# Softmax reciprocals on GpSimd as a power of minus one, and the two halves of the attention values added in place

## The chip, the cores and the metric

The kernel runs on one core of a Trainium2 chip. The metric is the device time of one execution in microseconds (us). TensorE is called PE, VectorE DVE, ScalarE ACT, GpSimd POOL, and SyncE, which issues the DMAs here, SP.

## The reference

One encoder layer on 1024 tokens with 1024 features, in float32: a conditioned RMSNorm, an input projection, two kinds of attention side by side (8 heads of latent attention, where a query sees all keys up to its own chunk of 64, and 8 heads of chunk attention, where it sees 9 chunks and a bias by relative position), an output projection, and a gated feed-forward part with a causal convolution. What the change touches is the softmax and what follows it, in both kinds of attention:

```python
    s = jnp.where(mask[None, None], s, NEG_INF)
    p = jax.nn.softmax(s, axis=-1).astype(v.dtype)
    return jnp.einsum('bqhk,bkhd->bqhd', p, v)
```

## The kernel before, in words

The work has four stages: the norm and the first projections (up to about 105 us of the span), attention with the other projections as filler (to about 670 us), the output projection (to about 745 us), and the feed-forward part. Every float32 matrix product is made of three products of high and low parts; the high part is a rounded copy made by ACT (L75), and the low part, the remainder, is made by POOL or DVE (L82).

Attention runs over 128 tiles. A tile is 128 queries of one head against all their keys (128 to 1024 of them); four tiles of a head form a unit. The 64 tiles of chunk attention come first (names with c: Pc, ric, hlc, PTc, pvc), then the 64 of latent attention (names with m). The method `scores` (L633) makes one tile:

- PE makes the scores in PSUM (L655), DVE their row minimum (L670 or L674; the sign is turned), and ACT the exponentials P with the row sum rsum beside them (L681).
- DVE makes ri, the reciprocal of rsum (L683), and scales it by 2^15 (L684).
- POOL makes the high half of the scaled probabilities in 16 bits, hl (L71, called at L702), and DVE the low half (L705). Rows of over 512 keys in latent attention are done in two pieces.
- SP issues a DMA that transposes hl into PT (L710).

Three tiles later the method `values` (L714) multiplies PT with the values in PE (L721). High and low parts of the values stand side by side, so the product pv has them on two halves of its 128 rows. After a unit's fourth tile ACT copies one half, scaled, from PSUM into the scratch tile sb (L728), DVE scales the other and adds sb to it into dst (L729), and SP stores dst (L730). Tiles sb and dst have one buffer each, rsum and ri four.

The filler is a list of generators that the loop over tiles (L822) runs between `scores` and `values`, by estimated costs: the other projections (L386, L395, L472), the two groups of latent up-projections (f_up, L517, with norms whose roots POOL makes as a power of -0.5: L115 and L116), and the output projection's half for chunk attention (f_oca, L595, whose weights and inputs are the tiles wo and cl). The program order so written is a proposal only: a list scheduler places the instructions of each engine and of SP's queue by data dependences, buffers and priorities, with modelled times (L1146). The scores have a higher priority (OFF_S) than the steps from the reciprocal on (OFF_P, L682) and the values (OFF_V). Within an engine the resulting order is fixed: an instruction that waits holds up all behind it.

## Time and profile before

| what | value |
|---|---|
| time, median of 3 runs | 1456.5 us (1454.95 to 1457.18) |
| the profiled execution | 1456.23 us, its span 1454.4 us |
| granted PE clock, mean | 0.936 |
| L683, L684 on DVE | 128 instructions each, medians 0.14 to 0.16 us |
| L71 on POOL | 160 instructions, 111.0 us |
| L728 on ACT, L729 on DVE | 32 each, medians 0.684 and 0.750 us |

All times in the views are counted from the span's start. A row of a group gives the source line, engine, operation, tiles written and read, shapes, the count, busy time and mean, then the engine's idle time before them and who ended it. A row of a source line gives shortest, median and longest duration in ns and the first and last start. A row of a wait gives who waited for whom, the us in total, the number of times and the longest. A row of the timeline gives start, length, engine, line, operation, and in brackets the idle time before it. A row of windows gives a stretch, its length and the busy time of each engine with the number of instructions, or of the instructions of one line alone.

### The profile page before, as it was taken

Reading aid. Unit: us, or ns where it says so; the run is one execution under the profiler, and the core shown is the slowest. Engines: PE = TensorE matmul, PEld = TensorE weight load, DVE = VectorE, ACT = ScalarE, POOL = GpSimd, SP = SyncE. Lnnn points to the kernel's source line nnn. Section 1 sums busy time; section 2 is a strip of 40 time slices with the busy share of each in tenths; the row PEclk is TensorE's granted clock in tenths of the full one; section 3 lists DMA queues with packets and bytes.
Section 4 is the critical chain, followed back from the end, with each engine's and each line's share of the span. In section 5 each row is a group of like instructions: output and inputs, shape, how many; then the busy total and the mean of one; then the engine's idle time right before and its main releaser. Section 6 shows DMA issues by size and latency. Waiting matters only on the chain.

```text
span 1454.4 us, 20116 instructions
## 1 busy us (share of the span) xinstructions
PE 1270.4 (87%) x6836; PEld 1054.4 (72%) x6836; DVE 1029.9 (71%) x1838; ACT 606.5 (42%) x1182; POOL 770.3 (53%) x717
## 2 busy tenths in 40 slices
PE   3859988998877789886668999999999998999997
PEld 2749877887765568675546877888888887887885
DVE  6964776576688988782577778778777776566653
ACT  4544344334455555452374343443444433322331
POOL 5363544265545764333735655556655555665662
PEclk9979997999887799997878999999999999999999
DMA  7423547555522588778712322322222234447442
GB/s 283 135 70 77 130 107 144 133 119 118 114 59 55 107 162 171 149 145 261 243 41 87 116 88 101 107 82 87 88 87 87 96 130 152 152 142 241 146 145 101
DMA packets 214627, 183.85 MB, mean 126 GB/s; under 512 B 148214, under 2 KB 179066, under 8 KB 213500
## 3 DMA queue, kind: packets, MB, share of 16 engines
q1 hardware_dynamic: 214524, 182.56, 45.3%
q8 instruction: 54, 0.88, 0.3%
q14 instruction: 49, 0.40, 0.1%
HBM read 119.07 MB, written 28.84 MB: 102 GB/s over the span
## 4 chain that ended last, share of the span: by engine, by line
PE 23%; POOL 9%; DVE 8%; issue 8%; DMA 7%; ACT 1%; SPq 1%; DVEq 0%; POOLq 0%; ACTq 0%
PE p L929 5%; PE p L931 5%; PE p L930 5%; POOL wds L82 5%; DMA wu<-w_up 2%; PE dnp L1072 2%; PE dnp L1074 2%; PE dnp L1073 2%; DVE u L1007 1%; DMA wd<-w_down 1%; DVE ws L1020 1%; DVE u L1006 1%; POOL wf L82 1%; POOL we L82 1%; POOL wd L82 1%
## 5 line engine op out<-in xcount | busy, mean ns | idle before, releaser
L82 POOL TENSOR_TENSOR wds<-wd,wds 128x512 fp32r<-128x512 f32 x88 | 152.4, 1753 | 102.7 <-ACT wds L75 102.7
L82 POOL TENSOR_TENSOR wc<-ws,wc 128x512 fp32r<-128x512 f32 x22 | 65.2, 2962 | 136.7 <-ACT wc L75 136.7
L1062 DVE TENSOR_TENSOR wd<-wd,gmbc 128x1024 f32<-128x1024 f32 x44 | 68.5, 1556 | 84.1 <-DMA wd<-w_down 84.0
L1074 PE MATMUL dnp<-wds,g 128*128 128x512 f32 x308 | 119.3, 393 | 4.6 <-DVE g L82 4.6
L1072 PE MATMUL dnp<-wds,g 128*128 128x512 f32 x308 | 120.0, 392 | 1.8 <-DVE xo L1080 1.7
L75 ACT ACTIVATE wds<-wd 128x512 fp32r<-128x512 f32 x88 | 54.8, 624 | 159.1 <-PE dnp L1074 152.3
L1073 PE MATMUL dnp<-wds,g 128*128 128x512 f32 x308 | 120.1, 391 | 0.0
L71 POOL TENSOR_SCALAR hlm<-Pm,rim 128x512 f16<-128x512 f32 (+3 forms) x96 | 64.8, 685 | 78.9 <-DVE rim L684 39.7
L71 POOL TENSOR_SCALAR hlc<-Pc,ric 128x640 f16<-128x640 f32 (+2 forms) x64 | 46.2, 724 | 80.6 <-DVE ric L684 39.5
L1020 DVE TENSOR_TENSOR ws<-wu,wu 128x512 f32<-128x512 f32 x22 | 30.5, 1387 | 75.0 <-DMA wu<-w_up 75.0
L681 ACT ACTIVATE Pc<-sc,mc 128x640 f32<-128x640 f32 (+2 forms) x64 | 42.2, 660 | 91.0 <-DVE mc L670 64.1
L655 PE MATMUL sm<-mk,mq 96*128 96x512 f32 (+3 forms) x288 | 71.2, 377 | 10.2 <-ACT Pm L681 6.7
L1006 DVE SCALAR_TENSOR_TENSOR u<-c,pk,u 128x1023 f32<-128x1023 f32 x44 | 77.4, 1766 | 1.8 <-ACT u L1005 1.8
L1041 ACT ACTIVATE u<-u 128x1024 f32<-128x1024 f32 x22 | 23.4, 1063 | 132.1 <-DVE u L1007 132.1
L655 PE MATMUL sc<-k,q 64*128 64x512 f32 (+3 forms) x288 | 68.7, 365 | 10.7 <-ACT Pc L681 6.8
L82 DVE TENSOR_TENSOR g<-gr,g 128x512 fp32r<-128x512 f32 x44 | 69.8, 1588 | 11.2 <-ACT g L75 11.2
L430 DVE SCALAR_TENSOR_TENSOR aacc<-aw,cs,aacc 128x256 f32<-128x256 f32 x84 | 44.1, 525 | 47.3 <-DMA aw<-w_ada 47.0
L1005 ACT ACTIVATE u<-c,pk 128x1024 f32<-128x1024 f32 x44 | 52.3, 1236 | 56.1 <-DVE c L1037 56.1
L705 DVE SCALAR_TENSOR_TENSOR hlm<-Pm,rim,hlm 128x512 f16<-128x512 f32 (+3 forms) x96 | 68.5, 727 | 6.1 <-POOL hlm L71 5.9
L721 PE MATMUL pvm<-PTm,vt 128*128 128x128 f16 x576 | 47.2, 232 | 28.6 <-DMA PTm<-hlm 24.5
L1074 PEld LDWEIGHTS dnp<-wds,g 128*128 128x128 f32 x308 | 58.2, 189 | 18.0 <-DVE g L82 5.9
L1072 PEld LDWEIGHTS dnp<-wds,g 128*128 128x128 f32 x308 | 58.1, 189 | 15.1 <-DVE xo L1080 2.6
(366 smaller groups left out, 4281.1 us busy)
## 6 DMA issues: line engine op xcount, KB each, us to landing
wu<-w_up SPq DMA_DIRECT2D x44, 512.0 KB, 4.5
wd<-w_down SPq DMA_DIRECT2D x44, 512.0 KB, 5.1
aw<-w_ada SPq DMA_DIRECT2D x96, 128.0 KB, 2.4
g_d<-u SPq DMA_DIRECT2D x22, 512.0 KB, 2.6
gr<-g_d SPq DMA_DIRECT2D x44, 256.0 KB, 3.6
x<-x SPq DMA_DIRECT2D x16, 512.0 KB, 6.6
adaw<-w_ada_a SPq DMA_DIRECT2D x8, 1024.0 KB, 5.2
wq_r<-w_qk SPq DMA_DIRECT2D x32, 128.0 KB, 2.8
```

The lines of the kernel that those rows point to most:

```text
L71: pool.tensor_scalar(o, i, s, 1.0, op0=MUL, op1=MUL)
L82: (pool if eng == "p" else dve).tensor_tensor(o, i, f32(hi), op=SUB)
L655: last = pe.matmul(s[:, c:c + w], qpg[rs_, a, q], kpgs[kh][rs_, b, ko:ko + w], start=(a == 0 and b == 0), stop=(a == 1))
L705: dve.scalar_tensor_tensor(hl[:, w:2 * w], pp, ri[:], hl[:, :w], op0=MUL, op1=SUB)
L929: pe.matmul(pt, sh, pg[:, 0], start=(k == 0), stop=False)
L930: pe.matmul(pt, sh, pg[:, 1], start=False, stop=False)
L931: pe.matmul(pt, sl, pg[:, 0], start=False, stop=(k == 3))
L1006: dve.scalar_tensor_tensor(u[:, 1:], c[:, :S - 1], pk[:, cv + 1:cv + 2], u[:, 1:], op0=MUL, op1=ADD)
L1062: dve.tensor_tensor(raw[:], raw[:], gmbc[:], op=MUL)
L1072: pe.matmul(pts[t][n], sh, w[n][:, 0], start=(j == 0), stop=False)
L1073: pe.matmul(pts[t][n], sh, w[n][:, 1], start=False, stop=False)
L1074: pe.matmul(pts[t][n], sl, w[n][:, 0], start=False, stop=(j == NF - 1))
```

## The change

The reciprocal is no longer made by DVE. POOL scales the row sum by 2^-15 and raises it to the power of -1, with a tile of -1 made once at the start. And ACT writes its half of the values straight into dst, to which DVE then adds the other half in place; the tile sb is gone. The scheduler places all instructions of the attention part anew; the numbers of lines shift by two from L102 on, and by one after the place where sb stood.

```diff
+    minus1 = cst.tile([P, 1], F32, name="minus1")
+    pool.memset(minus1[:], -1.0)
...
             with tc.high_priority(offset=OFF_P):
-                dve.reciprocal(ri[:], rsum[:, 0:1])
-                dve.tensor_scalar(ri[:], ri[:], PSCALE, None, op0=MUL)
+                pool.tensor_scalar(ri[:], rsum[:], 1.0 / PSCALE, 1.0, op0=MUL, op1=MUL)
+                pool.tensor_tensor(ri[:], ri[:], minus1[:], op=ALU.pow)
...
-                    sb = at.tile([P, 512], F32, name=f"sb{u.nm}_{u.g}", tag="sb", bufs=1)
                     dst = at.tile([P, 512], F32, name=f"o{u.nm}_{u.g}", tag="o", bufs=1)
                     r0, r1 = (slice(64, 128), slice(0, 64)) if u.odd else (slice(0, 64), slice(64, 128))
                     inv = vscale[u.vs][1]
-                    act.activation(sb[r0], u.pv[r1], AF.Copy, scale=inv[r1])
-                    dve.scalar_tensor_tensor(dst[r0], u.pv[r0], inv[r0], sb[r0], op0=MUL, op1=ADD)
+                    act.activation(dst[r0], u.pv[r1], AF.Copy, scale=inv[r1])
+                    dve.scalar_tensor_tensor(dst[r0], u.pv[r0], inv[r0], dst[r0], op0=MUL, op1=ADD)
                     sp.dma_start(u.dst_d[r0, u.g * 512:(u.g + 1) * 512], dst[r0])
```

## The prediction

> **What bounds the kernel now.** The page first: it says which engines are full on average.

> ```profile
> PE 1270.4 (87%) x6836; PEld 1054.4 (72%) x6836; DVE 1029.9 (71%) x1838; ACT 606.5 (42%) x1182; POOL 770.3 (53%) x717
> ```

> TensorE carries the kernel, but the diff touches only the attention part, and an average over the span says little of it. So I read busy time by stage next. The columns after the stretch and its length are PE, PEld, DVE, ACT and POOL, then granted clock, DMA share and GB/s.

> ```profile
> 105.00:405.00 300.00, 276.32 (x1965) 242.95 (x1964) 195.08 (x576) 124.88 (x335) 145.87 (x219) 0.93 0.54 117
> 405.00:435.00 30.00, 22.28 (x105) 16.95 (x104) 25.83 (x88) 15.94 (x40) 11.84 (x12) 0.83 0.25 56
> 435.00:520.00 85.00, 61.90 (x360) 49.49 (x361) 78.09 (x236) 47.36 (x111) 57.84 (x57) 0.82 0.43 93
> 520.00:670.00 150.00, 121.97 (x895) 100.59 (x892) 112.70 (x276) 70.04 (x148) 61.96 (x83) 0.93 0.80 160
> ```

> There are three stages. From 105 to 405 us (chunk attention with its projections) PE is busy 276.3 of 300 us: it bounds. From 435 to 520 us (latent attention together with its up-projections) DVE is busy 78.1 of 85 us, 92%, and PE only 61.9: DVE bounds, with POOL third at 57.8. From 520 to 670 us PE leads with 122.0 of 150 and nothing is full. The view of waits says how the reciprocal stands in this:

> ```profile
> POOL hlm L71 <- DVE rim L684: 39.7, 21, 4.8
> POOL hlc L71 <- DVE ric L684: 39.5, 18, 7.1
> ...
> PE pvm L721 <- DMA PTm<-hlm: 24.5, 19, 3.7
> ```

> POOL stands 79.2 us in all before its scaling of the probabilities (L71), until DVE has made the scalar ri; PE stands 24.5 us for the transposed probabilities that come of it. A tile in the timeline shows why:

> ```profile
> 493.65 1.01 ACT L681 ACTIVATE Pm<-sm,mm 128x896 f32<-128x896 f32 x1
> 493.75 0.15 DVE L683 RECIPROCAL rim<-rsm 128x1 f32<-128x1 f32 x1
> ...
> 498.81 0.14 DVE L684 TENSOR_SCALAR rim<-rim 128x1 f32<-128x1 f32 x1
> 498.88 0.27 DVE L467 TENSOR_TENSOR uqr<-qn,tabq 128x128 f32<-128x128 f32 x1
> 499.05 1.32 POOL L71 TENSOR_SCALAR hlm<-Pm,rim 128x512 f16<-128x512 f32 x2 [1.28 <-DVE rim L684]
> ```

> In DVE's order, 5 us of other work stand between one reciprocal and the next scaling. The same rows give the true price of such an instruction on DVE: L684 is recorded with 0.14 us, but the next instruction starts 0.07 us after it. Taking one away frees 0.07 us, not 0.15.

> **The change part by part.** The rows of the reciprocal in the three stages give the numbers of tiles:

> ```profile
> 105.00:405.00 300.00, 10.06 (x64) 0.93 0.54 117
> ...
> 435.00:520.00 85.00, 2.98 (x20) 0.82 0.43 93
> 520.00:670.00 150.00, 6.67 (x44) 0.93 0.80 160
> ```

> *Removed from DVE:* L683 and L684, 128 times each: 256 x 0.07 = 18 us of issue, of which 20 x 0.14 = 2.8 us in the stage that DVE bounds. The hop DVE to POOL goes too.

> *Added to POOL:* 128 times a scaling and a power, both 128x1. Before has no power of -1, but a power of -0.5 by the same instruction, and small scalings of the same kind:

> ```profile
> L115 POOL TENSOR_SCALAR ss<-ss x24: 191/198/1183, 79.8 to 741.4; 128x8 f32<-128x8 f32 x16, 128x1 f32<-128x1 f32 x8
> L116 POOL TENSOR_TENSOR rx<-ssx,nhalf x8: 549/551/566, 6.3 to 18.3; 128x1 f32<-128x1 f32 x8
> ...
> L344 POOL TENSOR_TENSOR vsm<-vsm,nhalf x2: 720/956/1191, 403.0 to 445.5; 128x1 f32<-128x1 f32 x2
> ...
> 435.00:520.00 85.00, 7.86 (x10) 0.82 0.43 93
> ```

> The low end is 0.19 + 0.55 = 0.74 us a tile. The last row is L115 (a scaling of 128x8) in the stage that matters: 7.86 / 10 = 0.79 us, four times its lowest. The power of 128x1 took 0.72 us at 445.5 and 1.19 us at 403.0. So the high end is 0.79 + 1.19 = 1.98 us, and I take the nearest rows by place, 0.79 + 0.72 = 1.51 us a tile from 435 to 520. The timeline shows POOL's instructions one after another with no overlap, so the price counts in full. The wait for the exponential's sum moves to POOL with it: behind it in POOL's order now stand the weights' remainders (L82), for which PE waits, and the up-projections' norms (L115, L116), for which DVE's L574 waits.

> [...]

> *Chunk attention, 64 tiles.* POOL would go from 145.9 to 145.9 + 64 x 1.51 = 242.5 of 300 us at most: still below PE's 276.3, and 39.5 us of POOL's waiting for ric go away. Value 0; bounds -3 (some of PE's 23.7 us of idle) to +4.

> *435 to 520 us, 20 tiles.* POOL gets 57.84 + 20 x 1.51 = 88.0 us of work in a stage that lasts 85: it takes DVE's place as the bound. If it idles as little as DVE does now (85 - 78.1 = 6.9 us), the stage lasts 94.9, or 9.9 us more. Some POOL work there can slide behind 520 us, where POOL has 88 us of room:

> ```profile
> L82 POOL TENSOR_TENSOR wo<-wor,wo 128x512 fp32r<-128x512 f32 x6 | 9.3, 1550 | 1.5 <-ACT wo L75 1.5
> ...
> L82 POOL TENSOR_TENSOR cl<-cl,ch 128x512 fp32r<-128x512 f32 x1 | 1.3, 1277 | 0.1
> ```

> If all 10.6 us slide, the stage ends 0.7 us early; if none, 9.9 late. The changed program's order on POOL keeps these between the tiles much as before, so I take the middle: +5. With the low price POOL has 72.6 us, DVE stays the bound and its 2.8 us come off: -3. With the high price POOL has 97.4 and the stage gains 19.

> *520 to 670 us, 44 tiles.*

> ```profile
> POOL hlm L71 <- DVE rim L684: 36.1, 19, 4.8
> ...
> PE pvm L721 <- DMA PTm<-hlm: 14.6, 11, 3.1
> ```

> POOL waited 19 times, 1.9 us each, for rim. At 0.79 to 1.51 us for the pair, a tile that waited gains 0.4 to 1.1 us (7.6 to 21 us in all) and the other 25 lose 0.8 to 1.5 us (20 to 38 us); POOL has 88 us free, so neither is the length of the stage. What counts is PE's 14.6 us of waiting for PTm. Value 0, bounds -6 (less than half of that goes) to +4.

> *The order.* The scheduler places things anew, in the attention part alone; from the feed-forward part on, the order is the same. One move stands out at the end: the loads of the first w_up page (SP, L938) and the two POOL remainders of it (wa, wb) go ahead of the last four tiles' scalars, and the first output-weight page (wo), which stood among those tiles, goes behind them.

> ```profile
> 652.56 2.37 POOL L71 TENSOR_SCALAR hlm<-Pm,rim 128x512 f16<-128x512 f32 x3 [2.36 <-DMA wor<-w_out]
> 654.90 1.56 POOL L82 TENSOR_TENSOR wo<-wor,wo 128x512 fp32r<-128x512 f32 x1
> ...
> 673.29 0.81 SPq L938 DMA_DIRECT2D wu<-w_up  x2
> ...
> 670.00:680.00 10.00, 9.37 (x28) 7.12 (x29) 1.22 (x1) 3.45 (x6) 5.08 (x4) 0.68 1.01 374
> ```

> Now POOL loses 2.4 us waiting and 1.6 us working there; after, it works on wa and wb and may wait for their load. One megabyte leaves the stretch where DMA is full (374 GB/s: 2.8 us) and joins the last transposes on SP's queue. Queued behind POOL's wait are the last tiles, their transposes, and the last values. Value 0, bounds -3 to +4.

> *The halves in place.* ACT now writes dst itself, so it waits for the previous store of dst, which DVE waited for before.

> ```profile
> 660.01 0.58 SPq L730 DMA_DIRECT2D oT_d<-om  x1
> ...
> 665.06 0.68 ACT L728 ACTIVATE sbm<-pvm,vabm 64x512 f32<-64x512 f32 x1 [11.37 <-PE pvm L721]
> ...
> DMA to landing us min/median/max: 2.2/2.4/2.7
> ```

> The tightest case seen is the last: the store's issue ends at 660.6, it has landed by 663.3, and ACT starts the next L728 at 665.06. Cover 1.8 us; cost 0. If a store is issued later still, ACT waits that long, with the exponentials queued behind it. The operations keep their shapes, so nothing is gained either; no other buffer uses the freed 2 KB.

> **Sum.** The profiled execution took 1456.2 us (span 1454.4), 0.3 below the median of 1456.5. 0 + 5 + 0 + 0 + 0 = +5: 1461.

> **The rivals.**
> 1. *Faster: the scalar comes sooner.* If the pair costs under 0.87 us (57.84 + 20 p below DVE's remaining 75.3), DVE stays the bound of 435 to 520 and gives 2.8 us; and PE's waits for PTm shrink, by 6 of 14.6 us. 1456 - 9 = 1447. For it: POOL's 79.2 us of waiting, and the low prices of 0.19 and 0.55. Against: 0.79 in the very stage.
> 2. *POOL bound further on.* From 520 to 570 us POOL has 25.5 us now, and 17 reciprocals stand there (second row):

> ```profile
> 520.00:570.00 50.00, 44.96 (x329) 37.76 (x327) 43.30 (x103) 26.25 (x55) 25.52 (x32) 0.97 0.84 157
> ...
> 520.00:570.00 50.00, 2.52 (x17) 0.97 0.84 157
> ```

> 25.52 + 17 x 1.51 = 51.2; with an idle share of 8% (6.9 / 85) 55.7, or 5.7 more, and nothing slides: 1456 + 9.9 + 5.7 = 1472. For it: DVE is still at 43.3 of 50 there, and POOL's small scalings were slow where DVE was fullest. Against: POOL would have to be slow with no up-projection beside it.
> [...]
> 4. *No difference.* The work that slides and the shorter chain cancel the fuller POOL: within 0.2%, 1456.

> **How the numbers follow.** Forecast (slower by 0.2 to 0.7%) 0.36, rival 1 0.31, rival 2 0.09, rival 3 0.07, rival 4 0.17. Faster 0.31, same 0.17, slower 0.52; 0.2%, about 3 us, is what a measurement of this kernel can tell from no change. The forecast's own range is 1459 to 1467. Both signs hold much of the chance, so the 8 in 10 reach into rivals 1 and 2: 1446 to 1474.

> **What would show it.** Right: the two new POOL groups together near 1.5 us a tile between 435 and 520, POOL above 90% there, DVE below 90%, the stage ending 3 to 10 us later, and no waits of L71 for rim. Wrong: the pair at 0.75 us and the stage shorter (rival 1); L705 or L578 much longer (rival 3); POOL full after 520 (rival 2). A difference that arises after 670 us would not be any of these, but the moved loads.

## The result, and the profile after

The changed kernel takes 1472.3 us (median of 4 runs, 1470.41 to 1479.97), the kernel before 1455.7 beside it: 1.0125 times as long, with a 95% interval from 1.0085 to 1.0165. That is 16.6 us slower, where +5 was forecast. Its profiled execution took 1470.48 us, its span 1468.7, which is 14.3 more than before.

The page of the changed kernel, then its busy times by stage, in the columns used above:

```profile
PE 1278.6 (87%) x6836; PEld 1058.3 (72%) x6836; DVE 1015.2 (69%) x1582; ACT 608.4 (41%) x1182; POOL 869.7 (59%) x974
```

```profile
105.00:405.00 300.00, 274.01 (x1954) 241.31 (x1954) 181.58 (x438) 122.39 (x328) 188.69 (x342) 0.92 0.50 116
405.00:435.00 30.00, 23.05 (x103) 18.41 (x103) 22.39 (x72) 15.69 (x37) 13.67 (x15) 0.70 0.24 60
435.00:520.00 85.00, 56.12 (x331) 43.81 (x330) 77.34 (x209) 46.78 (x111) 64.10 (x87) 0.87 0.32 76
520.00:670.00 150.00, 132.26 (x913) 108.00 (x914) 110.27 (x196) 73.85 (x155) 105.59 (x181) 0.92 0.70 158
```

POOL took on 99 us of work (770.3 to 869.7), DVE lost 15 us. But from 435 to 520 us POOL is busy 64.1 of 85 us, 75%, and DVE still 77.3, 91%: POOL did not become the bound. After 520 us POOL has 105.6 of 150. No engine but PE, and DVE in that one stage, is near full.

The two new lines in that stage, the scaling (L685) first and the power (L686) second, and their rows for all tiles:

```profile
435.00:520.00 85.00, 5.05 (x17) 0.87 0.32 76
```

```profile
435.00:520.00 85.00, 10.92 (x17) 0.87 0.32 76
```

```profile
L685 POOL TENSOR_SCALAR ric<-rsc x64: 183/190/792, 108.6 to 404.3; 128x1 f32<-128x1 f32 x64
L685 POOL TENSOR_SCALAR rim<-rsm x64: 183/191/1049, 442.0 to 668.5; 128x1 f32<-128x1 f32 x64
```

```profile
L686 POOL TENSOR_TENSOR ric<-ric,minus x64: 534/549/1507, 108.9 to 405.4; 128x1 f32<-128x1 f32 x64
L686 POOL TENSOR_TENSOR rim<-rim,minus x64: 538/549/1531, 442.6 to 668.8; 128x1 f32<-128x1 f32 x64
```

The pair costs (5.05 + 10.92) / 17 = 0.94 us a tile there, not 1.51: the power 0.64, the scaling 0.30. The medians, 0.19 and 0.55, are the low end of the prediction.

The waits of POOL and of DVE (who for whom, us, times, longest):

```profile
POOL ric L685 <- ACT Pc L683: 47.0, 28, 9.5
...
POOL rim L685 <- ACT Pm L683: 42.2, 25, 4.8
```

```profile
DVE hlm L707 <- POOL hlm L71: 22.9, 27, 2.1
DVE hlc L707 <- POOL hlc L71: 20.3, 22, 2.3
```

DVE's waits for the scaled copies before:

```profile
DVE hlc L705 <- POOL hlc L71: 6.7, 13, 0.9
DVE hlm L705 <- POOL hlm L71: 5.9, 11, 0.9
```

POOL's 79.2 us of waiting for DVE's scalar are gone, and 89.2 us of waiting for the exponential have come in their place. A wait that moves to another releaser is not a gain. And DVE waits 43.2 us for POOL's copy where it waited 12.6.

Where did the 14.3 us arise? The rows of the exponential give the first and the last start of the chunk tiles (Pc) and of the latent tiles (Pm). Before, and after:

```profile
L681 ACT ACTIVATE Pc<-sc,mc x64: 358/732/804, 106.6 to 401.6; 128x640 f32<-128x640 f32 x32, 128x128 f32<-128x128 f32 x8, 128x256 f32<-128x256 f32 x8, 128x384 f32<-128x384 f32 x8
L681 ACT ACTIVATE Pm<-sm,mm x64: 350/733/1121, 434.3 to 651.4; 128x128 f32<-128x128 f32 x8, 128x256 f32<-128x256 f32 x8, 128x384 f32<-128x384 f32 x8, 128x512 f32<-128x512 f32 x8
```

```profile
L683 ACT ACTIVATE Pc<-sc,mc x64: 361/730/798, 108.1 to 403.3; 128x640 f32<-128x640 f32 x32, 128x128 f32<-128x128 f32 x8, 128x256 f32<-128x256 f32 x8, 128x384 f32<-128x384 f32 x8
L683 ACT ACTIVATE Pm<-sm,mm x64: 354/733/1121, 441.5 to 667.2; 128x128 f32<-128x128 f32 x8, 128x256 f32<-128x256 f32 x8, 128x384 f32<-128x384 f32 x8, 128x512 f32<-128x512 f32 x8
```

The chunk tiles take 295.0 us before and 295.2 after; the handover from the last chunk tile to the first latent one 32.7 and 38.2; the latent tiles 217.1 and 225.7. Together +0.2 + 5.5 + 8.6 = 14.3 us, the whole of it; what lies ahead and behind is 909.6 us both times. The same three lengths serve for the experiments.

In the handover the trace shows where the time goes. POOL must scale the last rows of the latents (L490 and L491, in the changed kernel L492 and L493), on which the up-projections and so all latent tiles rest. These rows end at 400.2 instead of 390.4 us:

```profile
389.99 0.37 POOL L491 TENSOR_SCALAR lat<-lat,mr 128x128 f32<-128x128 f32 x1
```

```profile
399.31 0.92 POOL L493 TENSOR_SCALAR lat<-lat,mr 128x128 f32<-128x128 f32 x1
```

POOL can scale them only after ACT has copied the latents' product from PE and squared it. Before, ACT did this ahead of the next chunk tile's exponential:

```profile
383.26 0.52 ACT L481 ACTIVATE lat<-mp 128x416 f32<-128x416 f32 x1 [0.23 <-PE mp L152]
...
384.51 0.21 ACT L487 ACTIVATE msq<-lat 128x32 f32<-128x32 f32 x1
...
390.48 0.80 ACT L681 ACTIVATE Pc<-sc,mc 128x640 f32<-128x640 f32 x1 [5.66 <-DVE mc L670]
```

After, the product comes later, and the exponential goes first and waits 3.8 us for its row minimum:

```profile
389.27 0.52 ACT L483 ACTIVATE lat<-mp 128x416 f32<-128x416 f32 x1 [2.59 <-PE mp L154]
393.61 0.79 ACT L683 ACTIVATE Pc<-sc,mc 128x640 f32<-128x640 f32 x1 [3.82 <-DVE mc L672]
...
395.13 0.22 ACT L489 ACTIVATE msq<-lat 128x32 f32<-128x32 f32 x1
```

The last square ends at 395.35 instead of 384.72 us, 10.6 later: 6.0 of that is the later product, 4.6 the exponential ahead. From there POOL's last row takes 4.9 us, where it took 5.6, although POOL's pairs now stand among these rows. So the loss in the handover has to do with what PE and ACT take first, and the scheduler chose that. That makes two theories: the **price** of POOL's pair, or the **order** that the scheduler made when the pair was on POOL.

### The profile page after: what moved, and what is told of

The parts are those of the page before. It is cut to its first block, busy times and chain, and to the rows that moved or that the text cites. A ratio compares the mean times of both kernels' runs of the same rounds, so it can differ in the third digit from the quotient of the medians.

```text
span 1468.7 us, 20166 instructions
## 1 busy us (share of the span) xinstructions
PE 1278.6 (87%) x6836; PEld 1058.3 (72%) x6836; DVE 1015.2 (69%) x1582; ACT 608.4 (41%) x1182; POOL 869.7 (59%) x974
## 3 DMA queue, kind: packets, MB, share of 16 engines
q1 hardware_dynamic: 214524, 182.56, 43.2%
## 4 chain that ended last, share of the span: by engine, by line
PE 48%; DVE 15%; DMA 13%; POOL 12%; issue 7%; ACT 3%; SPq 1%; DVEq 0%; POOLq 0%; ACTq 0%
PE p L930 8%; PE p L932 8%; PE p L931 8%; DMA aw<-w_ada 5%; POOL wds L82 4%; PE sc L657 2%; PE dnp L1073 2%; PE dnp L1075 2%; PE dnp L1074 2%; DVE adacc L245 1%; DMA wu<-w_up 1%; POOL hlm L71 1%; DVE aacc L432 1%; PE sm L657 1%; PE ipv L152 1%
## 5 line engine op out<-in xcount | busy, mean ns | idle before, releaser
L82 POOL TENSOR_TENSOR wds<-wd,wds 128x512 fp32r<-128x512 f32 x88 | 151.9, 1746 | 103.1 <-ACT wds L75 103.1
L82 POOL TENSOR_TENSOR wc<-ws,wc 128x512 fp32r<-128x512 f32 x22 | 63.1, 2866 | 126.4 <-ACT wc L75 126.4
L75 ACT ACTIVATE wds<-wd 128x512 fp32r<-128x512 f32 x88 | 54.9, 624 | 160.3 <-PE dnp L1075 151.9
L82 DVE TENSOR_TENSOR g<-gr,g 128x512 fp32r<-128x512 f32 x44 | 70.0, 1592 | 11.4 <-ACT g L75 11.4
L1021 DVE TENSOR_TENSOR ws<-wu,wu 128x512 f32<-128x512 f32 x22 | 24.8, 1129 | 70.4 <-DMA wu<-w_up 70.4
L683 ACT ACTIVATE Pc<-sc,mc 128x640 f32<-128x640 f32 (+2 forms) x64 | 42.1, 658 | 72.0 <-DVE mc L672 58.4
L683 ACT ACTIVATE Pm<-sm,mm 128x128 f32<-128x128 f32 (+3 forms) x64 | 47.2, 738 | 54.9 <-DVE mm L676 39.1
L1075 PEld LDWEIGHTS dnp<-wds,g 128*128 128x128 f32 x308 | 57.8, 188 | 16.5 <-DVE g L82 4.5
L1073 PEld LDWEIGHTS dnp<-wds,g 128*128 128x128 f32 x308 | 57.8, 188 | 16.0 <-DVE xo L1081 3.4
L723 PE MATMUL pvm<-PTm,vt 128*128 128x128 f16 x576 | 50.2, 236 | 21.8 <-DMA PTm<-hlm 15.8
L657 PEld LDWEIGHTS sm<-mk,mq 96*128 96x128 f32 x288 | 49.8, 202 | 25.4 <-ACT Pm L683 16.9
```

Of the source, the lines that this page charges most:

```text
L82: (pool if eng == "p" else dve).tensor_tensor(o, i, f32(hi), op=SUB)
L657: last = pe.matmul(s[:, c:c + w], qpg[rs_, a, q], kpgs[kh][rs_, b, ko:ko + w], start=(a == 0 and b == 0), stop=(a == 1))
L683: act.activation(pr[:, :n], sv, AF.Exp, bias=m[:], scale=-1.0, accum_out=rsum[:, 0:1])
L1073: pe.matmul(pts[t][n], sh, w[n][:, 0], start=(j == 0), stop=False)
L1075: pe.matmul(pts[t][n], sl, w[n][:, 0], start=False, stop=(j == NF - 1))
```

## The experiments

Each is compared with the kernel before on the same chip. First, which edit it is.

**pool_only**: the reciprocals alone. **inplace_only**: the halves in place alone, with DVE's pair.

```diff
 pool_only, against before
-                dve.reciprocal(ri[:], rsum[:, 0:1])
-                dve.tensor_scalar(ri[:], ri[:], PSCALE, None, op0=MUL)
+                pool.tensor_scalar(ri[:], rsum[:], 1.0 / PSCALE, 1.0, op0=MUL, op1=MUL)
+                pool.tensor_tensor(ri[:], ri[:], minus1[:], op=ALU.pow)
 inplace_only, against before
-                    sb = at.tile([P, 512], F32, name=f"sb{u.nm}_{u.g}", tag="sb", bufs=1)
...
-                    act.activation(sb[r0], u.pv[r1], AF.Copy, scale=inv[r1])
-                    dve.scalar_tensor_tensor(dst[r0], u.pv[r0], inv[r0], sb[r0], op0=MUL, op1=ADD)
+                    act.activation(dst[r0], u.pv[r1], AF.Copy, scale=inv[r1])
+                    dve.scalar_tensor_tensor(dst[r0], u.pv[r0], inv[r0], dst[r0], op0=MUL, op1=ADD)
```

> The reciprocals on POOL, the scratch tile sb kept (the -1 shares a tile with the -0.5, for want of room). If all of the loss comes from the reciprocals (theory A: POOL pays 0.8 us a tile and holds up what stands behind it), 1470 to 1474 us, as the whole change. If ACT's wait for the store in place costs something (theory B), several us less than the whole change, 1460 to 1467.

> The halves added in place, reciprocals still on DVE. Theory A: as before, 1453 to 1459 us. Theory B: slower by the part that pool_only lacks, 1460 or more.

Measured: pool_only 1470.2 us, ratio 1.0119 (1.0099 to 1.0138); inplace_only 1450.9, ratio 0.9992 (0.9979 to 1.0005). The whole loss comes with the reciprocals, and the halves in place cost nothing.

**no_ri** makes no reciprocal at all, on neither engine, so that the probabilities are not normalised, and **mul_for_pow** has a multiplication in place of the power; both are the changed kernel otherwise.

```diff
 no_ri
-            ri = cst.tile([P, 1], F32, name=f"ri{nm}", tag="ri", bufs=4)
+            ri = minus1
...
-                pool.tensor_scalar(ri[:], rsum[:], 1.0 / PSCALE, 1.0, op0=MUL, op1=MUL)
-                pool.tensor_tensor(ri[:], ri[:], minus1[:], op=ALU.pow)
 mul_for_pow
-                pool.tensor_tensor(ri[:], ri[:], minus1[:], op=ALU.pow)
+                pool.tensor_tensor(ri[:], ri[:], minus1[:], op=MUL)
```

> The reciprocals are left out on both engines: the probabilities are scaled by a constant tile of -1, so the softmax is not normalised; all else as in the change. If the price on POOL is what counts (theory A1), the time lies below that of before, since DVE has 18 us less of issue and POOL nothing more: 1440 to 1450. If the loss is one of the order in which the scheduler places things once DVE has lost these instructions (theory A2), it stays above before: 1458 to 1472.

> The change with a product in place of the power (the scalar is then minus the scaled row sum, not its reciprocal): as many instructions on POOL with the same waits, each about 0.3 us shorter; the scheduler places things anew. Theory A1, price: the loss shrinks with the price from 0.82 to about 0.45 us a tile, to 1462 to 1467. Theory A2, the wait for the exponentials in POOL's queue whatever the price: 1468 to 1475.

Measured: no_ri 1453.6 us, ratio 1.0004 (0.9989 to 1.0019), outside the ranges on record; mul_for_pow 1461.2, ratio 1.0062 (1.0041 to 1.0082), just under the range that the price gave. With a cheaper instruction in the power's place half the loss is left, so price looks like a cause. But no_ri says more: taking 256 instructions off DVE, with the whole link between sum and scaled copy, gains nothing in the order that the scheduler made for it. Both kernels were ordered anew, so they do not part price from order. In mul_for_pow the loss lies in the chunk stage (first and last start 106.7 and 409.6 us, 7.9 us more than before).

**pool_c** and **pool_m** have POOL's pair for the chunk tiles or for the latent tiles only.

```diff
 pool_c, against after (pool_m has "if not u.band:")
-                pool.tensor_scalar(ri[:], rsum[:], 1.0 / PSCALE, 1.0, op0=MUL, op1=MUL)
-                pool.tensor_tensor(ri[:], ri[:], minus1[:], op=ALU.pow)
+                if u.band:
+                    pool.tensor_scalar(ri[:], rsum[:], 1.0 / PSCALE, 1.0, op0=MUL, op1=MUL)
+                    pool.tensor_tensor(ri[:], ri[:], minus1[:], op=ALU.pow)
+                else:
+                    dve.reciprocal(ri[:], rsum[:, 0:1])
+                    dve.tensor_scalar(ri[:], ri[:], PSCALE, None, op0=MUL)
```

> The change with POOL's reciprocals for the 64 chunk tiles only; the 64 latent tiles keep VectorE's pair. In place as in the change. The kernel before is about 1452 to 1456 us. If the loss lies where the milestones of the changed kernel put it (about nothing up to the end of the chunk tiles, 5.5 us in the handover at 400 to 440 us, and 10 us in the latent stage), this one has the handover's part: 1457 to 1460 us. If POOL's added time counts tile for tile wherever it is (64 of 128 tiles), half the loss: 1460 to 1464 us. If the order that the scheduler makes is the cause, no relation: anything from 1448 to 1475 us.

> The other half: POOL's reciprocals for the 64 latent tiles only, VectorE's pair for the chunk tiles. By the milestones it has the latent stage's part of the loss, 9 to 12 us: 1462 to 1466 us, and this and the run with the chunk tiles alone add up to the loss of about 17 us. By the count of tiles 1460 to 1464 us. If the order is the cause the two do not add up to it.

Measured: pool_c 1464.1 us, ratio 1.0087 (1.0056 to 1.0118); pool_m 1454.4, ratio 1.0019 (1.0004 to 1.0035). The split by the milestones (a third to pool_c, two thirds to pool_m) falls, and so does the even one, for pool_m lies 6 us under it: pool_c has most of the loss. The two losses, 11.6 and 1.9 us, add up to 13.5, less than the 18.1 of pool_only; that they need not add up is what the order theory said. The exponential's rows of pool_c:

```profile
L683 ACT ACTIVATE Pc<-sc,mc x64: 359/730/797, 105.4 to 401.0; 128x640 f32<-128x640 f32 x32, 128x128 f32<-128x128 f32 x8, 128x256 f32<-128x256 f32 x8, 128x384 f32<-128x384 f32 x8
L683 ACT ACTIVATE Pm<-sm,mm x64: 351/736/1122, 440.3 to 659.1; 128x128 f32<-128x128 f32 x8, 128x256 f32<-128x256 f32 x8, 128x384 f32<-128x384 f32 x8, 128x512 f32<-128x512 f32 x8
```

Chunk tiles 295.6 us (+0.6), handover 39.3 (+6.6), latent tiles 218.8 (+1.7): the chunk tiles' pairs are paid for in the handover. In pool_m the latent tiles lose 6.0 us, and most of that is made good by a chunk stage and a handover 6.4 us shorter; there its instructions are those of inplace_only, which had a chunk stage and a handover 3.1 us shorter than before. Lengths of stages come from one execution each: in inplace_only, as fast as before, the latent stage is 3.0 us longer, so differences of that size say little.

**pool_beside** leaves DVE's reciprocals and has POOL make the pair a second time, into a tile that nothing reads; **pool_twice** adds that unread pair to the changed kernel.

```diff
                             scale_pool(hl[:, :w], pp, ri[:])
...
+                        if x == 0:
+                            dd = cst.tile([P, 1], F32, name=f"dd{nm}", tag="dd", bufs=4)
+                            pool.tensor_scalar(dd[:], rsum[:], 1.0 / PSCALE, 1.0, op0=MUL, op1=MUL)
+                            pool.tensor_tensor(dd[:], dd[:], minus1[:], op=ALU.pow)
                         dve.scalar_tensor_tensor(hl[:, w:2 * w], pp, ri[:], hl[:, :w], op0=MUL, op1=SUB)
```

> VectorE makes the reciprocals as before, and POOL makes the same scaling and power a second time into a tile that nothing reads, right behind each tile's scaled copy: POOL has the added work of the change, and the chain from the exponential to the copy has the links of before. In place as in the change. If POOL's added occupancy is the cause (whatever stands behind it on POOL comes later), it costs as much as the change: 1466 to 1474 us. If the cause is that the link itself lies on the tile's chain (copy later behind its exponential), it costs nothing: 1449 to 1456 us. In between, both.

> The changed kernel with that second, unread scaling and power behind each tile's copy as well: POOL's added work doubled, the chain as in the change. If POOL's occupancy is the cause, the loss doubles or more (POOL is at 87 to 100 us of extra work in the attention already): 1484 to 1500 us. If the chain's link is the cause, the time stays near that of the changed kernel: 1468 to 1476 us.

Measured: pool_beside 1457.1 us, ratio 1.0038 (1.0026 to 1.005); pool_twice 1467.4, ratio 1.0112 (1.0085 to 1.0139). POOL's time alone costs a third of the loss, and twice the time costs no more than once: occupancy as such is not the measure. But again each has an order of its own (pool_twice's chunk stage, 107.4 to 398.4 us, is even 4.0 us shorter than before). So the order had to be held.

**pow_in_old_order** is the changed kernel with every instruction that the kernel before has too queued on its engine in the order of the kernel before; POOL's new pairs go where the scheduler finds them due. **old_in_pow_order** is the reverse: DVE's pairs, and all else in the order of the changed kernel.

```diff
+    for eng, order in json.loads(zlib.decompress(base64.b64decode(ORDER))).items():
+        own = [i for i in traced if str(i.engine) == "EngineType." + eng]
+        for x, y in zip(order, order[1:]):
+            tc.add_manual_dep(own[y], own[x].name,
+                              mybir.DependencyInfo(mybir.DependencyClass.NoSync, mybir.DependencyReason.DATA),
+                              reason="pin")
...
```

ORDER holds the other kernel's order for each engine.

> The changed kernel, POOL's scaling and power for all 128 tiles, but every instruction that the kernel before has too is queued on its engine in the order of the kernel before (TensorE, ScalarE, SyncE in full; VectorE without the pairs that are gone; POOL's with the two new ones let in where the scheduler finds them due). If the price and place of POOL's pair are the cause, the loss of the change stays: 1468 to 1475 us where the kernel before has 1452 to 1456. If the loss is the other order that the scheduler made when the pair was priced for POOL, it goes: 1450 to 1457 us. If the handover at 400 to 440 us is order and the latent stage is POOL's occupancy, as the milestones suggest, about half stays: 1459 to 1466 us.

> The other way round: reciprocals on VectorE as before (halves in place, which cost nothing), and every other instruction on each engine in the order of the changed kernel, with VectorE's pairs let in where they are due. If POOL's pair is the cause, no loss: 1449 to 1456 us. If the order is the cause, the loss is here: 1466 to 1474 us. If half is order (the handover), 1456 to 1463 us.

Measured: pow_in_old_order 1474.0 us, ratio 1.0113 (1.0091 to 1.0135); old_in_pow_order 1477.2, ratio 1.0161 (1.0139 to 1.0184). Each theory expected one of the two to be free of the loss, and neither is. The pair loses 17.8 us in the old order; the new order, with the old pair let into it, loses 21.0 us. The two do not add up in the changed kernel: there the order was made for the pair. No kernel was run that holds an order and changes nothing else, so what the holding itself costs was not measured; in the traces the instructions shared with the kernel whose order is held stand in its order on every engine.

The handover goes with the order. The exponentials of old_in_pow_order:

```profile
L681 ACT ACTIVATE Pc<-sc,mc x64: 347/734/798, 106.5 to 409.8; 128x640 f32<-128x640 f32 x32, 128x128 f32<-128x128 f32 x8, 128x256 f32<-128x256 f32 x8, 128x384 f32<-128x384 f32 x8
L681 ACT ACTIVATE Pm<-sm,mm x64: 355/734/1115, 448.9 to 680.1; 128x128 f32<-128x128 f32 x8, 128x256 f32<-128x256 f32 x8, 128x384 f32<-128x384 f32 x8, 128x512 f32<-128x512 f32 x8
```

With DVE's pair in the new order it is 39.1 us, 6.4 more than before; with POOL's pair in the old order it is 31.6. The chunk stage (303.3, +8.3) and the latent stage (231.2, +14.1) are longer too, in an execution that is the longest of its five, 6.9 us over their median.

The held old order shows what the pair costs where the scheduler does not move the rest. The exponential and the page of pow_in_old_order:

```profile
L683 ACT ACTIVATE Pc<-sc,mc x64: 352/731/799, 107.5 to 415.6; 128x640 f32<-128x640 f32 x32, 128x128 f32<-128x128 f32 x8, 128x256 f32<-128x256 f32 x8, 128x384 f32<-128x384 f32 x8
L683 ACT ACTIVATE Pm<-sm,mm x64: 349/732/1117, 447.2 to 670.5; 128x128 f32<-128x128 f32 x8, 128x256 f32<-128x256 f32 x8, 128x384 f32<-128x384 f32 x8, 128x512 f32<-128x512 f32 x8
```

```profile
PE 1288.1 (87%) x6836; PEld 1064.8 (72%) x6836; DVE 1009.3 (68%) x1582; ACT 606.7 (41%) x1182; POOL 876.9 (59%) x974
```

Chunk tiles 308.1 us (+13.1), handover 31.6 (-1.1), latent tiles 223.3 (+6.2): now the chunk stage pays. (This execution, too, is the longest of its five, 2.7 us over their median.) The chain of a tile, from the row sum's end on ACT to the end of the first low half on DVE (mean of 64 tiles, worked out from the trace's single rows), went from 3.82 to 4.24 us for chunk tiles and from 5.41 to 5.63 for latent ones. Is it that length, or POOL's time? Two more kernels in the held order ask this. **beside_in_old_order** is pool_beside in it. (In both, DVE's pairs go where the scheduler finds them due; all else stands in the old order.) **link_in_old_order** adds nothing to POOL and lengthens the chain by two small copies on ACT:

```diff
 link_in_old_order, against inplace_only
+                rib = cst.tile([P, 1], F32, name=f"rib{nm}", tag="rib", bufs=4)
+                act.activation(rib[:], rsum[:], AF.Copy)
+                act.activation(rib[:], rib[:], AF.Copy)
-                dve.reciprocal(ri[:], rsum[:, 0:1])
+                dve.reciprocal(ri[:], rib[:])
```

> All instructions that the kernel before has in its own order on every engine, VectorE's reciprocals among them; POOL makes the scaling and the power a second time into a tile that nothing reads, let in behind each tile's copy. With the order held, POOL's own pair in the chain cost 1.1% (1474 us against 1456). If that is POOL's occupancy (latents' rows, squares and weights behind it on POOL come later), the loss is here too: 1466 to 1475 us where the kernel before has 1452 to 1456. If it is the link in each tile's chain, it goes: 1450 to 1458 us. In between, both; then TensorE's busy time at the same 6836 matmuls, 1270 us before and 1288 with the pair in the chain, moves with it.

> The same held order with no work added on POOL or VectorE: ScalarE copies each tile's row sum twice (128x1) between the exponential and VectorE's reciprocal, so that the chain is longer by some 0.4 us a tile, as POOL's pair made it (4.94 against 4.61 us from the exponential to the low halves' end). If the link is the cause: 1464 to 1474 us. If POOL's occupancy is the cause, next to nothing: 1451 to 1459 us (ScalarE is 42% busy).

Measured: beside 1471.2 us, ratio 1.0104 (1.008 to 1.0129); link 1495.2, ratio 1.0265 (1.0247 to 1.0283). Each theory expected one of the two to be free, and neither is: beside lies in the range that POOL's occupancy gave, and link lies above even the range that the link gave. So neither theory holds alone as put. The exponentials of beside, then those of link:

```profile
L683 ACT ACTIVATE Pc<-sc,mc x64: 347/731/797, 106.0 to 406.8; 128x640 f32<-128x640 f32 x32, 128x128 f32<-128x128 f32 x8, 128x256 f32<-128x256 f32 x8, 128x384 f32<-128x384 f32 x8
L683 ACT ACTIVATE Pm<-sm,mm x64: 348/731/1117, 440.1 to 666.2; 128x128 f32<-128x128 f32 x8, 128x256 f32<-128x256 f32 x8, 128x384 f32<-128x384 f32 x8, 128x512 f32<-128x512 f32 x8
```

```profile
L681 ACT ACTIVATE Pc<-sc,mc x64: 348/733/797, 107.4 to 424.1; 128x640 f32<-128x640 f32 x32, 128x128 f32<-128x128 f32 x8, 128x256 f32<-128x256 f32 x8, 128x384 f32<-128x384 f32 x8
L681 ACT ACTIVATE Pm<-sm,mm x64: 348/732/1120, 456.9 to 690.7; 128x128 f32<-128x128 f32 x8, 128x256 f32<-128x256 f32 x8, 128x384 f32<-128x384 f32 x8, 128x512 f32<-128x512 f32 x8
```

Put beside the length of the chain, which grew in beside too (POOL's unread pair stands ahead of later copies), the three go the same way:

| held order | chain longer, 64 chunk tiles | chunk stage longer | chain longer, 64 latent tiles | latent stage longer |
|---|---|---|---|---|
| pair on POOL | 64 x 0.42 = 27 us | 13.1 | 64 x 0.22 = 14 us | 6.2 |
| unread pair beside | 64 x 0.08 = 5 us | 5.8 | 64 x 0.32 = 20 us | 9.0 |
| two copies on ACT | 64 x 0.75 = 48 us | 21.7 | 64 x 0.64 = 41 us | 16.7 |

But for one small entry (5.8 for 5), each us by which the chain grew goes with 0.4 to 0.5 us of stage, whichever engine lengthened it, and link left POOL's work as it was. So in the old order the loss goes along with the length of the tile's chain from sum to low half. That the length is the cause is argued, not shown: in beside it is POOL's time that lengthens the chain, a tile that comes late for another reason lengthens it too, and ACT's copies add 0.4 us a tile to ACT (medians 0.202 and 0.203 us), which is 43% busy; what part of link's loss that is was not tried.

In the new order the rule does not come out. Old_in_pow_order has the changed kernel's order with DVE's pair for POOL's: its chunk chain is 4.49 us for 4.39, its latent chain 4.75 in both, yet its chunk stage is 8.1 us longer than the changed kernel's and its latent stage 5.5.

Where the scheduler orders each kernel anew, the stage does not go with the chain at all: the chunk stage is 295.5 us with a chain of 2.42 (no_ri), 302.9 with 3.82, the same as before (mul_for_pow), 295.2 with 4.39 (the changed kernel), and 291.0 with 6.66 (pool_twice). And the changed kernel's latent chain is shorter than before, 4.75 for 5.41 us, though its latent stage is 8.6 us longer. So the move of the reciprocals is shown to be the source of the changed kernel's loss, and the handover's 5.5 us are shown to go with the new order. Why the latent stage is longer stays open.

## Why the prediction was right in sign and wrong in its steps

- **POOL becomes the bound of 435 to 520 us (+5): this step failed.** The pair took 0.94 us a tile there, not 1.51, and POOL came to 75%, not 104%; DVE stayed ahead of it with 91%. The stage did lose some time: its first tile came 7.2 us late (434.3 and 441.5), and the tile that starts at 519.1 us before came 11.0 late (530.1), so 3.8 us arose between. That this is near +5 is luck, since the reason given for it did not arise. The prediction took the price from rows that stood in a crowded moment; the medians over the trace, 0.19 and 0.55, were nearer.
- **A price under the limits of an engine is hidden (chunk tiles 0, 520 to 670 us 0): half wrong.** The chunk tiles came out (+0.2), but only in the order made for the pair: with the old order held they lost 13.1 us (bounds -3 to +4), with POOL at 186 of 300 us. And the tiles that start after 520 us before lost 4.8 more by the last one (15.8 late). The bounds were set by comparing an engine's busy time with the length of the stage; in the held order the runs showed a loss though no engine but PE was near full, and one that grew with the tile's chain. For the latent tiles the chain did become shorter, and the stage is longer all the same.
- **The order (0, bounds -3 to +4): the term most out of size.** That the scheduler places all anew was said, but only the loads at the end were looked at. The order made for POOL's pair cost 21.0 us when the pair was taken out of it. The place that the trace shows, the last latents' product and squares later on PE and ACT (handover +5.5), was not foreseen; the end of the attention, which was, gave nothing: the time ahead and behind the tiles stayed at 909.6 us.
- **The number.** The measured 1472.3 us lies inside 1446 to 1474, at its edge, and the sign is right; with the terms above as they came out, that is luck more than reading.
- **The halves in place (0): right,** 0.9992 (0.9979 to 1.0005). (The time to landing counts from the issue's start, so the store had landed by 662.7 us at most, and the cover was 2.4 us, not 1.8.)
- **DVE's 18 us of freed issue:** without any reciprocal the time is 1.0004 of before, so in the order made for that kernel they were worth nothing. DVE's one stage as the bound, worth 2.8 us in rival 1, did not show.
- **The rivals.** Rival 1 (faster with a pair under 0.87 us) missed its condition narrowly, at 0.94 in the stage, but what the condition stood for came: DVE stayed the fuller engine, 77.3 us to POOL's 64.1, and the kernel still lost. Rival 2 named 1472 us, the time that came, for a reason that did not hold: POOL is busy 105.6 of 150 us after 520. Rival 3 was to show in L705 much longer; DVE's low halves kept their length, 0.728 us in the median before and 0.738 after, so DVE was not held up by the power. Before and after:

```profile
L705 DVE SCALAR_TENSOR_TENSOR hlm<-Pm,rim,hlm x96: 264/728/1776, 437.3 to 657.6; 128x512 f16<-128x512 f32 x48, 128x128 f16<-128x128 f32 x16, 128x256 f16<-128x256 f32 x16, 128x384 f16<-128x384 f32 x16
```

```profile
L707 DVE SCALAR_TENSOR_TENSOR hlm<-Pm,rim,hlm x96: 267/738/1629, 447.4 to 671.2; 128x512 f16<-128x512 f32 x48, 128x128 f16<-128x128 f32 x16, 128x256 f16<-128x256 f32 x16, 128x384 f16<-128x384 f32 x16
```

But a hold does show the other way round: POOL is held up by DVE. A low half on DVE that ends at 606.82 us, and a power on POOL that starts under it and ends at 607.23, 0.41 us later:

```profile
606.07 0.75 DVE L707 SCALAR_TENSOR_TENSOR hlm<-Pm,rim,hlm 128x512 f16<-128x512 f32 x1 [0.24 <-POOL hlm L71]
```

```profile
606.32 0.91 POOL L686 TENSOR_TENSOR rim<-rim,minus 128x1 f32<-128x1 f32 x1
```

In the changed kernel's trace, 18 powers start under a low half that runs for at least 0.2 us more: each ends 0.40 to 0.42 us after that low half, and they take 0.90 us on average. The 69 powers with no DVE operation running on so long over their start take 0.55 us on average, and the 15 that start under a reduction on DVE, which has one input, 0.55 in the median. Of 27 scalings that start under such a low half, 24 end 0.05 us after it. From 435 to 520 us it shows beside DVE's TENSOR_TENSOR operations (qn, kn, uqr) as well: counting these with the low halves, six powers of 0.61 to 0.86 us end 0.40 to 0.41 us after one of them, and four scalings of 0.35 to 1.05 us end 0.05 us after one. So POOL's small operations were slow there beside DVE's two-input ones, and the pair took 0.94 us in that stage and not 0.74. In the other direction the power shows no hold (of DVE's low halves of 128x512 that start under a power of the pair, all six take 0.73 to 0.75 us), but POOL's copies hold DVE: in the kernel before, 12 of the 13 low halves of 128x512 that start under a copy that runs for at least 0.2 us more end 0.54 us after it, and they take up to 1.17 us.

What stays open: how much of the changed kernel's loss is order and how much the pair's price cannot be told as two sums, since each order fits one pair. No version here beats the kernel before; no_ri, which makes no ri at all, does not either. Whether another order would was not tried.

## What to carry to other kernels

Where tiles pass through a chain of engines, an instruction moved in that chain can cost time though its engine has a third of its time free (here 17.8 us in the old order, with POOL busy 186 of 300 us of the chunk stage): ask what feeds on the chain, not only which engine is full. Where a scheduler places the instructions, a dearer operation also buys a new order, and its loss shows up elsewhere (here in the handover to the next stage). To part the two, hold the order of the kernel before and change the operation alone, and hold it once with nothing changed, as the control that is missing here.

## What the runs showed of the hardware

TensorE's busy time did not tell its work here. With the order held, these are the first 300 us of attention with POOL's pair; before, the same stretch had 276.32 us at 1965 matmuls and a granted clock of 0.93:

```profile
105.00:405.00 300.00, 275.25 (x1909) 240.87 (x1909) 175.06 (x423) 117.14 (x317) 186.07 (x331) 0.91 0.46 110
```

PE was as busy as before, 24.8 us idle against 23.7, and did 56 matmuls fewer, in the same order. The loss is hardly in the view of waits: PE's waits there for the transposed probabilities went from 9.4 to 8.2 us (before, then with the pair in the held order).

```profile
PE pvc L721 <- DMA PTc<-hlc: 9.4, 8, 2.3
```

```profile
PE pvc L723 <- DMA PTc<-hlc: 8.2, 8, 2.4
```

The clock is not the whole of it. With two copies on ACT 66.6 us of the chunk stage are at half, which by the same estimate accounts for 12 of its 21.7 us; PE's idle time grew by 10.6. And the mean grant did not set the time: on the same chip two executions of the kernel before with a mean of 0.927 and 0.928 took 1456.17 and 1456.37 us, and one with the pair in the held order and a mean of 0.931 took 1468.31. Why there were more half-clock stretches at about the same idle time was not tried.
